# Seven block products in place of eight for f 6 to 16 only, in the first three feed-forwards of a two-layer diffusion step

## The chip, the cores and the metric

The kernel runs on one core of one Trainium2 chip. The metric is the time of one execution on the device in microseconds. A profile of one execution gives the times of single instructions; its span runs from the first to the last instruction. TensorE multiplies matrices, VectorE, ScalarE and GpSimd work on elements, SyncE's queue issues the transfers.

## The reference, cut to what matters

Two layers over 640 tokens (128 context, 512 latent) of width 1024. Each layer has a half-step feed-forward, a token mixer (attention in the first layer, Fourier mixing in the second) and another half-step feed-forward, so there are four feed-forwards of inner width 2816.

```python
def modulate(x, shift, scale):
    return x * (1.0 + scale[:, None, :]) + shift[:, None, :]

def swiglu(h, w_gate, w_up, w_down):
    return (jax.nn.silu(h @ w_gate) * (h @ w_up)) @ w_down

def half_ffn(x, shift, scale, gate, w_gate, w_up, w_down, g, b):
    h = modulate(x, shift, scale)
    return post_norm(x, FFN_HALF * swiglu(h, w_gate, w_up, w_down), gate, g, b)
```

The shifts, scales and gates are nine vectors a layer, each a product of the conditioning vector with a 1024 x 1024 part of `w_ada`.

## The kernel before, in words

The whole step is one program. Activations lie transposed: features on the 128 partitions, the 640 tokens along the row, in two halves (half 0 of 254 or 256 columns, half 1 of 386 or 384). Every float32 product is made of three: each operand is split into a high part (rounded to the matrix format) and a low part (the rest), and high x high, high x low and low x high are summed in PSUM (`mm3`, line 506). A high part is a cast, mostly on ScalarE; a low part is a subtraction on VectorE or GpSimd.

The method `ffn` (line 962) writes one feed-forward. The inner width is 22 blocks f of 128 columns. They are taken in groups (`THREES`, line 38): f 0 to 2, 3 to 5, 6 to 8, 9 to 11, 12 to 14, 15 and 16, 17 and 18, 19 to 21. The list `units` is the order of TensorE's work:

- `gk` and `g`: gate or up product of a block in the plain form, for one half, over the 8 row blocks of the weights. One block needs four such units, 4 x 24 matrix products.
- `s`: gate and up of a block for all tokens in seven block products in place of eight (Strassen's scheme in Winograd's form, `strassen`, line 1370). Gate and up of two row halves make a 2 x 2 block matrix with the two token halves of 320 columns. Seven products of 4 x 3 matrix products each; the weights need four sums and seven splits (`weights`), the activations the factors T1 to T4, made once (`form`), and the results five operations on VectorE before the low part of the hidden value (`gate_a`, `up_b`, `gate_b`, `kept`).
- `d`: down projection of a whole group for some of the 8 output blocks; it reads the hidden values (tiles `hd`), and VectorE adds it into `ya` with the gate (`add_out`).

Before the change a block is taken in the seven-product form if it is neither among the first three or four nor among the last two: f 4 to 19 in the first feed-forward, f 3 to 19 in the other three. Group g's down projection follows the first block of the next group. A list of loads with due times (`todo`) feeds four raw buffers through SyncE's queue. In the first three feed-forwards it also holds the loads of the modulation weights (40, 32 and 40 of 512 KB). Each is read twice on VectorE (`matvec`, line 538: the rows `junk<-raw,cond,bada`, followed by a read of the accumulator). The last feed-forward has none of them.

The order on each engine is fixed when the program is written: a planner with a clock per engine (`Queue`, line 179, `step`, line 404) hands each waiting piece of work to the engine that would have it done first. `end_t` is the unit from which loads for the next stage may start and late weights may use spare tiles; the last group's first down projection is preceded by the affine of the next stage (`affine`, line 622), which needs the modulation vectors of that stage.

Of the kernel before, what the change touches and what calls it, by code (L numbers as in the profile page):

```python
# [12 lines left out]
F32R = mybir.dt.float32r  # L13
# [10 lines left out]
NT = NP + NS  # L24
# [11 lines left out]
FT = DFF // 128  # L36

THREES = ((0, 3), (3, 3), (6, 3), (9, 3), (12, 3), (15, 2), (17, 2), (19, 3))
# [140 lines left out]
class Queue:  # L179
# [41 lines left out]
    def run(self, aps, outs, dur):  # L221
        c = self.clock
        t = max([self.t] + [self.after(x) for x in aps])
        outs = [x for x in outs if x is not None]
        for x in outs:
            t = max(t, c.free.pop(x.tensor.name, 0))
        self.t = t + dur
        for x in outs:
            c.written(x, self.t, self.name)
        for x in (*aps, *outs):  # L230
            c.in_use(x, self.t + 200)
# [51 lines left out]
class Step:  # L283
# [675 lines left out]
        place, when = lambda: ops.take(only=only), lambda: ops.free(2, only)  # L959
        return [(self.io["w_gu"][l, j, n // 2, n % 2], self.block(dst, n, place, when)) for n in range(m)]  # L960

    def ffn(self, l, j, i, nxt, pool, ops, gu, first, groups, ada=0, urgent=0, after=(), early=False, reserve=True, **kw):

# [11 lines left out]
        self.clock.exact(True)  # L977
        start, order = self.order, ORDER
        self.order = order
        plain = 4 if early else 3  # L980
        fast = lambda f: plain <= f < FT - 2
        last = len(groups) - 1
        units, held = [], []
        for g, (f0, n) in enumerate(groups):
# [5 lines left out]
            if g == last or g == 1 and not urgent:  # L990
                units, held = units + held, []
            for f in range(max(f0, 2 if early else 3), f0 + n):
# [4 lines left out]
                if f == f0:  # L997
                    units, held = units + held, []
# [11 lines left out]
        for t, u in enumerate(units):  # L1010
# [8 lines left out]
            for k in ks:  # L1019
                use.setdefault(k, [t, t])[1] = t  # L1020
            begins.append(begins[-1] + dur)
        fasts = [t for t, u in enumerate(units) if u[0] == "s"]
        end_t = fasts[-1] + 1

        tickets, graw, dn, wf, todo, dnx = deque(), {}, {}, {}, [], [0]

# [117 lines left out]
        for a in range(ada):  # L1144
            src, fn = self.ada_load()
            t = int(np.searchsorted(at, 0.95 * clock * (a + 0.5) / ada))
# [2 lines left out]
        todo.sort(key=lambda t: t[0])  # L1149
        gate = self.lnp.tile([128, KT, 2], F32, name="gate", bufs=2)  # L1150
        hid, hidden_by = {}, set()
        hids = Slots(pool, "hd", 2 * max(n for _, n in groups), [128, NT], F32R)
        sts, here, ready = [{}, {}], [0], []
        h, xs = self.h, self.xs
        self.ada_live = 0
# [26 lines left out]
        forms, formed = {}, []  # L1182
# [166 lines left out]
        pending = []  # L1349
# [11 lines left out]
        def flush(n=2):  # L1361
            while pending and n:
                fn, *args = pending.pop(0)
                fn(*args)
                n -= 1
            if formed and not pending and here[0] >= end_t:
                self.xt.give(*formed)
                formed.clear()

        def strassen(f):  # L1370
            st = {}
            st["b1"] = self.take()[:, :HALF]
            product(st["b1"], f, "A11", b11, True)
            self.spawn(snap(st, "p1", st["b1"]), first=1)
            st["b2"] = self.take()[:, :HALF]
            product(st["b2"], f, "S1", t1, True)
            flush(1)
            self.need(lambda: "p1" in st)
            product(st["b1"], f, "S2", t2, False)
            self.spawn(snap(st, "u2", st["b1"]), first=1)  # L1380
            st["b3"] = self.take()[:, :HALF]
            product(st["b3"], f, "A12", b21, True)
            self.spawn(gate_a(f, st), first=1)
            flush(1)
            self.need(lambda: "u2" in st)
            product(st["b1"], f, "S3", t3, False)
            self.spawn(up_b(st), first=1)
            pending.extend([(p4, f, st), (p3, f, st)])
# [18 lines left out]
        for t, u in enumerate(units):  # L1407
            here[0] = t
            half = u[1]
            n = self.n[half]  # L1410
# [6 lines left out]
            elif u[0] == "g":  # L1417
# [7 lines left out]
                else:  # L1425
                    self.spawn(hidden(u[2], half, pg, ps))
                flush()
            elif u[0] == "s":
                strassen(u[2])
            else:  # L1430
                _, _, outs, g = u
# [981 lines left out]
    def run(self):  # L2413
        io = self.io
        got = {}
        with ExitStack() as ctx:
            spill = ctx.enter_context(self.tc.tile_pool(name="spill", bufs=1, space=bass.MemoryType.DRAM))
            saved = [spill.tile([128, NT], F32, name=f"sp{o}") for o in range(KT)]
            psums = ExitStack()
            self.psum(psums)  # L2420
            self.ada_open(ctx)
            with ExitStack() as sctx:
                self.x_slots(sctx)
                pool = self.ffn_pool(sctx)
                ops = self.work_slots(pool, 10, True)
                self.start(ops)
                free_w = lambda: sum(map(is_w, ops.rest)) == 4 or bool(got)
                after = [(io["w_ab"][n], self.block(got, n, self.wtile, free_w)) for n in range(2)]
                after += [(io["w_ab"][n], lambda t, n=n: got.update({n: t})) for n in (2, 3)]
                self.ffn(0, 0, 0, (0, 3), pool, ops, {}, 0, THREES, 40, 8, after, True, spill=saved, kept=False)  # L2430
            got, old = {}, got
            self.spawn(self.ada_beside(16), first=-2)
            self.mixer_ab(old, got, psums)
            fin = {}
            self.psum(ctx)
            self.x_slots(ctx)
            with ExitStack() as sctx:
                pool = self.ffn_pool(sctx)
                ops = self.work_slots(pool, 10, False)
                old = {}  # L2440
                self.ab_out(1, 0, ops, saved, self.first_blocks(0, 1, old, ops, 5), got, ORDER[::-1])
                got = {}
                self.ffn(0, 1, 2, (1, 0), pool, ops, old, 5, THREES, 32, 0, self.first_blocks(1, 0, got, ops, 2, is_w))
                self.ffn(1, 0, 3, (1, 3), pool, ops, got, 2, THREES, 40, after=[self.fin_block(n, fin) for n in range(3)], reserve=False, plain=True)
            with ExitStack() as sctx:
                fx = self.pool(sctx, "fx")
                parts = self.mixer_f(fin, fx)
                pool = self.ffn_pool(sctx)
                ops = self.work_slots(pool, 10, False)
                got = {}  # L2450
                self.f_out(4, 1, parts, fx, ops, self.first_blocks(1, 1, got, ops, 5))
                self.ffn(1, 1, 5, None, pool, ops, got, 5, THREES, reserve=False)
                self.drain()

def layouts(inputs):
# [144 lines left out]
```

## Time and profile before

| | us |
|---|---|
| median of 3 runs | 2534.91 |
| lowest and highest run | 2534.05, 2539.28 |
| profiled execution | 2540.61 |
| its span | 2538.7 |
| TensorE busy with products | 2343.9 |
| VectorE busy | 2091.6 |
| ScalarE busy | 1006.7 |
| GpSimd busy | 641.1 |

Busy times are sums over the span of the profiled execution; the stages of the program differ in what limits them, so the shares of a stretch say more than those of the whole. In tables by stretch the columns give the busy time of an engine with its number of instructions in brackets, the granted TensorE clock as a share of full speed, and the transfers. In lists in order of time the columns are start, duration, engine, line, operation, output and inputs, shapes and count; brackets give the idle time just ahead and who ended it.

### The profile page before, as it was taken

The page shows a single profiled execution, that of the slowest core. Times are in us where ns is not written, and L with a number is a line of the kernel's source. Part 1 is how long each engine was busy: PE and PEld are TensorE (multiplying, and loading weights), DVE is VectorE, ACT ScalarE, POOL GpSimd, SP SyncE. Part 2 cuts the span into 40 slices and gives each one's busy share as a digit, 9 for nine tenths or more (in the row PEclk, how much of TensorE's full clock was granted, in tenths as well). Part 3 has the DMA queues.
Part 4 walks back from the last instruction along what each step waited for, and adds up shares of the span by engine and source line. Part 5 has one row for each costly group of instructions (what it writes and reads, how often), then busy time and mean ns, then how long its engine had stood idle before and what let it go on. Part 6 is the DMA issues. An engine that isn't in the chain of part 4 may idle for free. (4 is left out here: it accounts for less than half of the span.)

```text
span 2538.7 us, 40214 instructions
## 1 busy us (share of the span) xinstructions
PE 2343.9 (92%) x14909; PEld 2231.7 (88%) x14909; DVE 2091.6 (82%) x4254; ACT 1006.7 (40%) x2212; POOL 641.1 (25%) x601
## 2 busy tenths in 40 slices
PE   7899999889989998999999889999996998999997
PEld 6899999888668898999998889999985788999996
DVE  7878888879767778889887898889889788777766
ACT  3333434243556634434442434333324344444432
POOL 7501012252322333011221621011325552000001
PEclk7999999989799998999999989999997999999998
DMA  6423333523122211433334033333334201222211
GB/s 243 133 84 117 117 125 125 161 85 112 46 59 68 72 66 63 133 117 117 119 123 133 25 117 119 114 126 116 119 115 163 96 33 60 76 87 88 90 61 42
DMA packets 98564, 258.03 MB, mean 102 GB/s; under 512 B 15224, under 2 KB 28216, under 8 KB 98368
## 3 DMA queue, kind: packets, MB, share of 16 engines
q1 hardware_dynamic: 98368, 255.45, 30.9%
q8 instruction: 118, 1.93, 0.3%
q14 instruction: 78, 0.64, 0.1%
HBM read 247.79 MB, written 5.52 MB: 100 GB/s over the span
## 5 line engine op out<-in xcount | busy, mean ns | idle before, releaser
L463 PE MATMUL a<-hh,wu 128*128 128x320 f32 (+4 forms) x2312 | 555.3, 314 | 14.0 <-POOL wu L200 7.9
L463 PE MATMUL a<-hd,wu 128*128 128x386 f32 (+3 forms) x2712 | 468.1, 316 | 24.0 <-DVE tmp L200 8.5
L200 ACT CAST wu<-raw 128x512 fp32r<-128x512 f32 (+1 forms) x482 | 303.0, 650 | 431.4 <-DVE raw L200 149.4
L463 PEld LDWEIGHTS a<-hd,wu 128*128 128x128 f32 x2712 | 424.0, 193 | 27.8 <-DVE tmp L200 9.0
L463 PEld LDWEIGHTS a<-hh,wu 128*128 128x128 f32 x2312 | 404.7, 192 | 16.5 <-POOL wu L200 8.2
L463 PE MATMUL a<-xt,wu 128*128 128x320 f32 (+2 forms) x2456 | 392.1, 313 | 19.8 <-ACT tmp L200 9.9
L463 PEld LDWEIGHTS a<-xt,wu 128*128 128x128 f32 x2456 | 369.3, 190 | 26.8 <-ACT tmp L200 13.6
L200 DVE CUSTOM_DVE_ANT_0 junk<-raw,cond,bada 128x1024 bf16<-128x1024 f32 x256 | 358.9, 1402 | 23.0 <-DMA raw<-in_w_ada 20.7
L463 PE MATMUL a<-hl,wu 128*128 128x320 f32 (+4 forms) x1140 | 357.9, 314 | 8.9 <-POOL hl L200 7.8
L200 DVE SCALAR_TENSOR_TENSOR ya<-a,gate,ya 128x128 f32<-128x128 f32 (+3 forms) x768 | 298.2, 432 | 70.6 <-PE a L463 67.1
L200 DVE TENSOR_TENSOR wu<-raw,wu 128x512 fp32r<-128x512 f32 (+1 forms) x412 | 309.4, 762 | 29.1 <-ACT wu L200 25.6
L463 PE MATMUL a<-hh,w 128*128 128x320 f32 (+6 forms) x1056 | 266.0, 318 | 2.1 <-ACT hh L200 2.1
L463 PE MATMUL a<-hd,w 128*128 128x254 f32 (+3 forms) x1320 | 247.2, 314 | 12.2 <-ACT hd L200 9.1
L200 POOL TENSOR_TENSOR wu<-raw,wu 128x512 fp32r<-128x512 f32 (+1 forms) x70 | 112.4, 1611 | 516.6 <-ACT wu L200 370.0
L463 PEld LDWEIGHTS a<-hl,wu 128*128 128x128 f32 x1140 | 218.9, 192 | 10.9 <-POOL hl L200 8.6
L463 PEld LDWEIGHTS a<-hd,w 128*128 128x128 f32 x1320 | 209.3, 191 | 13.9 <-ACT hd L200 9.8
L200 ACT CAST w<-raw 128x512 fp32r<-128x512 f32 (+3 forms) x222 | 139.9, 638 | 179.1 <-DVE raw L200 52.6
L463 PEld LDWEIGHTS a<-hh,w 128*128 128x128 f32 (+1 forms) x1056 | 186.5, 191 | 5.9 <-ACT hh L200 3.4
L200 POOL TENSOR_TENSOR w<-raw,w 128x512 fp32r<-128x512 f32 (+3 forms) x58 | 86.6, 1495 | 403.6 <-ACT w L200 361.3
L463 PE MATMUL a<-hl,w 128*128 128x320 f32 (+6 forms) x544 | 172.1, 316 | 1.8 <-POOL hl L200 1.6
L463 PE MATMUL a<-xt,w 128*128 128x320 f32 (+2 forms) x1016 | 166.3, 314 | 5.1 <-ACT tmp L200 5.1
L463 PEld LDWEIGHTS a<-xt,w 128*128 128x128 f32 x1016 | 154.5, 192 | 8.3 <-ACT tmp L200 6.3
(443 smaller groups left out, 3446.2 us busy)
## 6 DMA issues: line engine op xcount, KB each, us to landing
raw<-in_w_gu SPq DMA_DIRECT2D x176, 512.0 KB, 4.4
raw<-in_w_ada SPq DMA_DIRECT2D x128, 512.0 KB, 3.7
raw<-in_w_dn SPq DMA_DIRECT2D x176, 256.0 KB, 3.1
raw<-in_w_fin SPq DMA_DIRECT2D x16, 520.0 KB, 4.5
raw<-in_w_ab SPq DMA_DIRECT2D x11, 512.0 KB, 4.5
xt<-in_w_ada SPq DMA_DIRECT2D x8, 512.0 KB, 7.5
raw<-in_w_abo SPq DMA_DIRECT2D x8, 512.0 KB, 4.0
raw<-in_w_fout SPq DMA_DIRECT2D x8, 512.0 KB, 4.1
```

The lines of the kernel that those rows point to most:

```text
L200: return getattr(self.engine, op)(*args, **kw)
L463: pe.engine.matmul(out, w, x, **kw)
```

## The change

A new parameter `seven` names the blocks that are taken in the seven-product form: f 6 to 16 where nothing is said, f 3 to 19 in the call for the last feed-forward. In the first three, f 3 (or 4) to 5 and f 17 to 19 become plain units. `end_t` is now taken from the first unit of f 19, whatever its form, and the factors of the blocks are given back after the last seven-product block. The number of hidden tiles is written as 6, which it was.

```diff
-    def ffn(self, l, j, i, nxt, pool, ops, gu, first, groups, ada=0, urgent=0, after=(), early=False, reserve=True, **kw):
+    def ffn(self, l, j, i, nxt, pool, ops, gu, first, groups, ada=0, urgent=0, after=(), early=False, reserve=True, seven=(6, 17), **kw):
...
-        plain = 4 if early else 3
-        fast = lambda f: plain <= f < FT - 2
+        fast = lambda f: seven[0] <= f < seven[1]
...
-        fasts = [t for t, u in enumerate(units) if u[0] == "s"]
-        end_t = fasts[-1] + 1
+        seven_t = max(t for t, u in enumerate(units) if u[0] == "s") + 1
+        end_t = min(t for t, u in enumerate(units) if u[0] in "gs" and u[2] == FT - 3) + 1
...
-        hids = Slots(pool, "hd", 2 * max(n for _, n in groups), [128, NT], F32R)
+        hids = Slots(pool, "hd", 6, [128, NT], F32R)
...
-            if formed and not pending and here[0] >= end_t:
+            if formed and not pending and here[0] >= seven_t:
...
-                self.ffn(1, 1, 5, None, pool, ops, got, 5, THREES, reserve=False)
+                self.ffn(1, 1, 5, None, pool, ops, got, 5, THREES, reserve=False, seven=(3, FT - 2))
```

The order of the instructions moves on every engine, since the planner places all of them anew. Three places follow.

TensorE, second feed-forward, where the down projection of group 0 (it reads the hidden tiles `hd`) ends and block f 3 begins (it reads the activations' high and low parts `hh` and `hl`). Before:

```order
L463 MATMUL a_10654<-hd_10217,w_10313 128x386
L463 MATMUL a_10654<-hd_10218,w_10313 128x386
L463 MATMUL a_10654<-hd_10217,w_10313 128x386
L463 MATMUL a_10667<-hh_78,wu_10366 128x320
L463 MATMUL a_10667<-hl_86,wu_10366 128x320
L463 MATMUL a_10667<-hh_78,wu_10366 128x320
```

Now:

```order
L463 MATMUL a_10578<-hd_10162,w_10258 128x386
L463 MATMUL a_10578<-hd_10163,w_10258 128x386
L463 MATMUL a_10578<-hd_10162,w_10258 128x386
L463 MATMUL a_10590<-hh_78,wu_10309 128x386
L463 MATMUL a_10590<-hl_86,wu_10309 128x386
L463 MATMUL a_10590<-hh_78,wu_10321 128x386
```

Block f 3 starts with a product of half 1 (386 columns) with a high and a low weight tile of their own, where a product of 320 columns with one tile for both parts stood.

VectorE, third feed-forward, ahead of the first down projection of the last group: from the low part of the second last hidden product to that of the last (`ISA junk` is a modulation product, `ISA mod` its accumulator, `affa` and `affb` the affine of the next stage). Before:

```order
L200 TENSOR_TENSOR hd_19254<-tmp_19245,hd_19253 128x386
L200 ISA junk,mod_8_14753<-raw_19201,cond,bada 128x1024
...
L200 ISA junk,mod_8_14753<-raw_19267,cond,bada 128x1024
...
L200 ISA junk,mod_8_14753<-raw_19287,cond,bada 128x1024
...
L200 TENSOR_SCALAR affa<-mod_4_14749 128x16
...
L200 TENSOR_TENSOR tmp_19320<-tmp_19320,a_19282 128x386
L200 ISA junk,mod_8_14753<-raw_19309,cond,bada 128x1024
L200 ISA mod_8_14753 128x1
L200 TENSOR_TENSOR hd_19352<-tmp_19320,hd_19351 128x386
```

Now:

```order
L200 ISA junk,mod_8_14632<-raw_19006,cond,bada 128x1024
L200 ISA mod_8_14632 128x1
L200 TENSOR_TENSOR tmp_19084<-tmp_19084,a_19058 128x386
L200 TENSOR_TENSOR hd_19092<-tmp_19084,hd_19091 128x386
L200 TENSOR_TENSOR raw_19141<-raw_19141 128x2x256
L200 TENSOR_TENSOR raw_19143<-raw_19143 128x520
L200 TENSOR_TENSOR raw_19145<-raw_19145 128x2x256
L200 TENSOR_TENSOR tmp_19150<-tmp_19150,a_19116 128x386
L200 TENSOR_SCALAR affa<-mod_4_14628 128x16
```

The five modulation products between the two hidden products and the one behind the last multiplication are gone from there: the last one of the feed-forward now stands ahead of the second last hidden product. Three sums of the next stage's weights have come in, and the affine stands behind the last multiplication; its low part is on GpSimd.

VectorE, third feed-forward, ahead of the first output of group 0's down projection: from the low part of the second last hidden product of half 0 to the last. Before:

```order
L200 TENSOR_TENSOR hd_15105<-tmp_15297,hd_15104 128x254
L200 TENSOR_TENSOR wu_15314<-raw_15292,wu_15314 128x512
L200 TENSOR_TENSOR raw_15292<-raw_15292 128x512
L200 TENSOR_TENSOR raw_15290<-raw_15292,raw_15290 128x512
...
L200 TENSOR_TENSOR wu_15362<-raw_15290,wu_15362 128x512
L200 TENSOR_TENSOR wu_15373<-raw_15292,wu_15373 128x512
L200 TENSOR_TENSOR wu_15375<-raw_15290,wu_15375 128x512
L200 TENSOR_TENSOR raw_15290<-raw_15290,raw_15292 128x512
L200 TENSOR_TENSOR tmp_15383<-tmp_15383,a_15300 128x254
...
L200 TENSOR_TENSOR hd_15152<-tmp_15383,hd_15151 128x254
```

Now:

```order
L200 TENSOR_TENSOR hd_14984<-tmp_15181,hd_14983 128x254
L200 TENSOR_TENSOR xt_15216<-tmp_15088,xt_15216 128x320
L200 TENSOR_TENSOR xt_15216<-tmp_15089,xt_15216 128x320
L200 ISA junk,mod_4_14628<-raw_15240,cond,bada 128x1024
L200 ISA mod_4_14628 128x1
L200 TENSOR_TENSOR tmp_15247<-tmp_15247,a_15174 128x254
```

The sums and low parts of the weights of block f 3 are gone; the low parts of the factors (`xt`) have come together there.

## Rows read from the trace of the kernel before

**Rows 1.** The page's first part: busy us, share of the span, instructions.

```profile
PE 2343.9 (92%) x14909; PEld 2231.7 (88%) x14909; DVE 2091.6 (82%) x4254; ACT 1006.7 (40%) x2212; POOL 641.1 (25%) x601
```

**Rows 2.** Busy times by stretch: the four feed-forwards behind group 0, in their order.

```profile
core 0: us, PE busy (x) PEld busy (x) DVE busy (x) ACT busy (x) POOL busy (x), PEclk, DMA share, GB/s
136.00:526.00 390.00, 369.76 (x2460) 365.39 (x2458) 333.01 (x625) 139.54 (x274) 59.44 (x45) 0.98 0.37 120
1019.00:1409.00 390.00, 380.03 (x2545) 376.85 (x2543) 334.21 (x638) 144.78 (x286) 62.58 (x45) 0.99 0.36 119
1505.00:1908.00 403.00, 385.63 (x2543) 381.58 (x2542) 348.03 (x652) 141.93 (x284) 64.84 (x49) 0.97 0.36 119
2137.00:2516.00 379.00, 376.93 (x2550) 374.83 (x2548) 268.63 (x529) 141.59 (x285) 22.57 (x17) 1.00 0.22 72
```

**Rows 3.** TensorE in order of time: the two ends of the last feed-forward's stretch.

```profile
2137.43 0.31 PE L463 MATMUL a<-hh,wu 128*128 128x320 f32 x1
...
2515.31 0.52 PE L463 MATMUL a<-hd,wu 128*128 128x254 f32 x3
```

**Rows 4.** TensorE in order of time: 36 products of 320 columns and the next one.

```profile
327.19 5.44 PE L463 MATMUL a<-xt,wu 128*128 128x320 f32 x36
332.47 0.31 PE L463 MATMUL a<-hh,w 128*128 128x320 f32 x1
```

**Rows 5.** TensorE in order of time: waits in the first and third feed-forward.

```profile
343.29 0.56 PE L463 MATMUL a<-xt,wu 128*128 128x320 f32 x2 [3.61 <-ACT wu L200]
...
490.96 0.69 PE L463 MATMUL a<-hd,xt 128*128 128x384 f32 x1 [6.86 <-ACT hd L200]
...
1482.53 0.58 PE L463 MATMUL a<-hd,w 128*128 128x254 f32 x1 [6.25 <-ACT hd L200]
...
1869.69 0.44 PE L463 MATMUL a<-hd,w 128*128 128x386 f32 x1 [2.90 <-ACT hd L200]
```

**Rows 6.** VectorE in order of time, ahead of the last of these waits' end.

```profile
1864.42 2.19 DVE L200 CUSTOM_DVE_ANT_0 junk<-raw,cond,bada 128x1024 bf16<-128x1024 f32 x1
...
1868.54 0.55 DVE L200 TENSOR_TENSOR tmp<-tmp,a 128x386 f32<-128x386 f32 x1
1869.01 1.28 DVE L200 CUSTOM_DVE_ANT_0 junk<-raw,cond,bada 128x1024 bf16<-128x1024 f32 x1
...
1870.21 1.61 DVE L200 TENSOR_TENSOR hd<-tmp,hd 128x386 fp32r<-128x386 f32 x1
```

**Rows 7.** Busy times by stretch (columns of rows 2): behind that wait, and undisturbed.

```profile
1870.00:1880.00 10.00, 8.26 (x32) 8.12 (x32) 7.13 (x12) 0.00 (x0) 1.91 (x2) 0.66 0.18 52
2200.00:2210.00 10.00, 10.00 (x66) 10.00 (x65) 9.26 (x22) 3.01 (x6) 0.00 (x0) 1.00 0.08 33
```

**Rows 8.** VectorE's groups by form: busy us, mean ns, then idle before.

```profile
L200 DVE TENSOR_TENSOR wu<-raw,wu 128x512 fp32r<-128x512 f32 x387 | 276.0, 724 | 26.2 <-ACT wu L200 24.3
L200 DVE TENSOR_TENSOR raw<-raw,raw 128x512 f32<-128x512 f32 x181 | 129.9, 718 | 16.7 <-DMA raw<-in_w_gu 11.3 <-issue 1.6 <-POOL raw L200 1.2
L200 DVE TENSOR_TENSOR tmp<-a,tmp 128x320 f32<-128x320 f32 x201 | 97.9, 488 | 53.6 <-PE a L463 42.6 <-ACT tmp L200 9.8
L200 DVE TENSOR_TENSOR hd<-tmp,hd 128x320 fp32r<-128x320 f32 x125 | 63.1, 513 | 10.2 <-ACT hd L200 9.9
L200 DVE TENSOR_TENSOR wu<-raw,wu 128x1024 fp32r<-128x1024 f32 x25 | 33.5, 1355 | 2.9 <-PE a L463 1.6 <-ACT wu L200 1.3
L200 DVE TENSOR_TENSOR hd<-tmp,hd 128x386 fp32r<-128x386 f32 x14 | 10.3, 735 | 4.0 <-ACT hd L200 3.9
L200 DVE TENSOR_TENSOR tmp<-tmp,a 128x386 f32<-128x386 f32 x15 | 8.2, 550 | 8.2 <-PE a L463 8.2
```

**Rows 9.** Waits, longest in total, from 440 to 505 us: ScalarE for a load.

```profile
ACT w L200 <- DMA raw<-in_w_ab: 6.9, 2, 5.6
```

**Rows 10.** The page's part on DMA issues: KB each, us to landing.

```profile
raw<-in_w_gu SPq DMA_DIRECT2D x176, 512.0 KB, 4.4
```

## The prediction, made before the change was run

> **What bounds the kernel now.** I read the profile's first part, then a table of the four feed-forwards by stretch of time, then the rows that end TensorE's waits inside them. The first part gives no clear owner: matrix products are busy 92% of the span, weight loads 88%, VectorE 82% [rows 1]. The table does [rows 2]. Each of its stretches runs from the first product after group 0's down projection to the last product of the last group. The last feed-forward has the same units as the second and third, but no modulation products beside it, and its stretch lasts 379 us at a granted clock of 1.00; its two ends are in [rows 3]. The second takes 390 us, the third 403. The first starts one seven-product block later, which is 84 products of 320 columns at (332.47 - 327.19) / 36 = 0.147 us [rows 4], or 12.3 us; so its measure is 367 us, and it takes 390. Against the undisturbed stretch the three lose 23 + 11 + 24 = 58 us. VectorE's busy share of the undisturbed time tells why: 269 / 379 = 71% in the last, but 333 / 367 = 91%, 334 / 379 = 88% and 348 / 379 = 92% in the first three. TensorE needs all the time there, VectorE nearly all.
>
> TensorE's own waits agree: 3.61 us for a cast weight in mid-stage, 6.86 and 2.90 us for the last hidden product [rows 5]. What stood ahead of that hidden product in the third feed-forward is in VectorE's rows: a modulation product of 2.19 us, the eight small operations of the next affine, the multiplication itself only at 1868.54, another modulation product, and only then its low part [rows 6]. TensorE had been ready since about 1866.8. Such a wait costs twice: in the 10 us around it TensorE got through 32 products at a clock of 0.66, against 66 at 1.00 in a full stretch [rows 7].
>
> **What the change costs.** A block in the seven-product form takes 7 x 12 = 84 products of 320 columns; in the plain form 48 of 384 or 386 columns and 48 of 256 or 254, 30,720 columns for 26,880. That is 12 products of 320 more, 12 x 0.147 = 1.76 us [rows 4]. Seventeen blocks change: f 4, 5, 17, 18, 19 in the first feed-forward (f 2 and 3 were plain), f 3 to 5 and 17 to 19 in the second and third. The instruction order has 204 products more, which agrees. **+29.9 us** on TensorE. I count all of it, since TensorE has no spare time in those stretches.
>
> **What it takes from VectorE.** A seven-product block has 4 weight sums, 7 low parts of 512 columns, 5 operations on products and 2 low parts of the hidden values: 4 x 0.718 + 7 x 0.724 + 5 x 0.488 + 2 x 0.513 = 11.4 us. A plain one has 2 low parts of 1024, 2 multiplications and 2 low parts of the hidden values, at most 2 x 1.355 + 2 x 0.550 + 2 x 0.735 = 5.3 us [rows 8]. That is 6.1 us a block if all of it stands on VectorE. Some of both stands on GpSimd, whose order has 44 instructions fewer. In VectorE's order 155 instructions go; form by form with the means of the trace that is 70 us, some 23 us a feed-forward. ScalarE has 141 instructions fewer and is busy 40% of the span [rows 1]: worth nothing. The transfers are the same 715 issues; what moves is when the modulation loads come.
>
> If 19 of the 23 us lie inside the stretch, VectorE's share of the time that TensorE now needs (376, 389 and 389 us) falls to 84%, 81% and 84%. The four stretches of before give 0 us lost at 71%, 11 at 88%, 23 and 24 at 91 and 92%. A straight line from the first to the second gives 6 to 9 us at the new shares; the points bend upward beyond, so a little less is likely: I take 6 each. **58 - 18 = 40 us come back.** The ends: all 58 come back (the last feed-forward's level), or none.
>
> The end of each stretch is the surest part. In the order of before, six modulation products and the affine stand between the last two hidden products; after the change all of them stand ahead of the second last, and what is left in front of the last one is a few casts or sums of weights. The 6.86 and 2.90 us should shrink to the chain's own latency of one to three. The clock comes back with them.
>
> **The start of the third feed-forward.** TensorE waits 6.25 us there for the last hidden product of group 0 [rows 5]. Between the last two hidden products' low parts VectorE's order now lacks 4 low parts of weights and 3 weight sums, 4 x 0.724 + 3 x 0.718 = 5.1 us, and gains up to 2 us in larger pieces of the factors' and weights' splits moved ahead of it. I take **-3 us**, between 0 and -5. The second feed-forward shows no such wait, and the first waits there for its eight urgent modulation products, which stay.
>
> The last feed-forward keeps its seven-product blocks. The factors of the blocks are given back after f 16, so late down-projection weights find room sooner (96 more of their products read such a slot): nothing, since no wait of before is for a slot.
>
> **Sum.** +29.9 - 40 - 3 = -13 us. The profiled execution took 2540.6 us (span 2538.7 and 1.9 around it), so it would be 2527. It was 5.7 us above the median of the three runs, 2534.9, from which **2521 us** follows. Some 0.2% (5 us) is what a measurement of this kernel can tell from no change.
>
> **A rule against the change.** In VectorE's share I see the cause, though TensorE's weight loads have the higher share of the span, 88% to 82% [rows 1], and 382 of 403 us of the third stretch [rows 2]. The Trainium skill (Perfetto Trace Analysis, Identifying the Most-Contended Engine) says to judge TensorE by the share of its weight loads and VectorE by its busy time, and to work on the engine with the highest first. By it, adding products to TensorE brings only their 29.9 us.
>
> **Rivals.**
> - *TensorE bounds these stretches, and the waits are latency.* A hidden product passes from TensorE through ScalarE, VectorE, ScalarE and VectorE again before the down projection can read it, in the plain form as in the other. If the waits at the heads of groups come from that chain and not from VectorE's queue, they stay, and the change costs up to 29.9 us: 2565 us. It decides where fewer than 30 us of the 58 come back. Against it: the last feed-forward has the same chain and loses nothing. Chance 0.10. It is the case that the skill's rule describes.
> - *A transfer takes the modulation's place.* In the new order VectorE's casts, low parts or sums of the next stage's weights stand right ahead of the last hidden product, and each waits for its load. Such a load was late by 5.6 us on ScalarE before [rows 9], where it blocked nobody; 512 KB take 4.4 us to land [rows 10]. In the order the up product of f 20, 48 products of 386 columns with its gate (some 8 us at the rate of [rows 4]), lies between the release of a raw buffer and that place and should hide it. Also, between the first outputs of the groups of f 15 and f 17 up to 11 modulation products now stand: VectorE's order times the means gives some 30 us there, TensorE's work 27.6 us. Then some 13 us each stay lost: 58 - 39 = 19 come back, +29.9 - 19 - 3 = +8: 2543 us. Chance 0.20.
> - *All lost time comes back*, to the level of the last feed-forward: 29.9 - 58 - 5 = -33: 2502 us. Chance 0.12.
>
> That the change doesn't do what it says is excluded by the order: the blocks named are plain in it, 204 products more.
>
> **How the numbers follow.** My forecast has 0.58. Its own range is 2513 to 2534 (between 3 and 10 us left in each stretch). The range takes in the best case and the second rival, **2502 to 2544**; what is left out is the first rival's upper part and the tails. Faster by over 5 us: 0.53 of my forecast, all of the best case, 0.02 of the second rival, **0.67**. Within 5 us: 0.05 + 0.07 + 0.02 = **0.14**. Slower: 0.11 + 0.08 = **0.19**.
>
> **What would show it.** Right: the three stretches last about 382, 395 and 395 us (undisturbed 376, 389, 389 and 6 each), the last stays at 379; no modulation product stands between the multiplication and the low part of the last hidden product, and TensorE's wait there is under 3 us; VectorE's total falls by some 60 us or more, TensorE's count of products rises by 204. Wrong: stretches of over 400 us, with waits on loads or on ScalarE's casts at the heads of the last groups, or granted clocks of 0.66 still there.

## The result, and the profile after

The changed kernel takes 2501.56 us (median of four runs, 2494.91 to 2504.22), the kernel before beside it 2536.71 us (2534.05 to 2539.28): ratio 0.9858, 95% interval 0.9834 to 0.9881. That is 35 us less. Faster was forecast, but 13 to 14 us, and the measured time lies just under the lower end of the range. Measured again later, the same two gave 0.9837 [0.9812, 0.9862].

The profiled execution has a span of 2501.3 us, against 2538.7. The page's first part, which answers to [rows 1]:

```profile
PE 2356.0 (94%) x15113; PEld 2248.9 (90%) x15113; DVE 2011.3 (80%) x4099; ACT 948.5 (38%) x2071; POOL 574.2 (23%) x557
```

TensorE has 204 products more, as the order said, and VectorE is busy 80 us less (70 were forecast). The four feed-forwards behind group 0, in the columns of [rows 2]:

```profile
131.00:509.00 378.00, 372.11 (x2520) 369.55 (x2519) 313.44 (x581) 123.04 (x238) 56.44 (x44) 1.00 0.38 123
1005.00:1397.00 392.00, 388.91 (x2618) 386.91 (x2616) 311.33 (x588) 125.17 (x243) 45.12 (x34) 1.00 0.35 115
1488.00:1878.00 390.00, 387.37 (x2616) 384.78 (x2614) 326.86 (x613) 125.48 (x242) 52.41 (x38) 1.00 0.38 123
2100.00:2478.00 378.00, 376.10 (x2546) 374.21 (x2545) 268.37 (x528) 141.05 (x284) 22.56 (x17) 1.00 0.23 72
```

All four now have a granted clock of 1.00. The four waits in [rows 5] are gone or under 1 us. In the first feed-forward the last hidden product's low part now ends a wait of 0.16 us, where its high part ended one of 6.86:

```profile
476.95 4.28 PE L463 MATMUL a<-hd,xt 128*128 128x384 f32 x23 [0.16 <-POOL hd L200]
```

At the start of the third, the wait for the last hidden product of group 0, 6.25 us in [rows 5], is 0.76 us. The wait just ahead of it, for the second last hidden product, stays: 3.79 us before (first fence), 4.45 us after (second fence, which shows both).

```profile
1471.61 0.58 PE L463 MATMUL a<-hd,wu 128*128 128x254 f32 x1 [3.79 <-ACT hd L200]
```

```profile
1460.98 0.58 PE L463 MATMUL a<-hd,wu 128*128 128x254 f32 x1 [4.45 <-ACT hd L200]
...
1466.54 2.07 PE L463 MATMUL a<-hd,w 128*128 128x254 f32 x8 [0.76 <-POOL hd L200]
```

At the end of the third, VectorE stood idle 4.97 us ahead of the multiplication that [rows 6] had at 1868.54, and the affine now runs behind it while GpSimd makes the low part; no modulation product stands there. The second fence below is the 10 us that answer to [rows 7]: 57 products at a clock of 1.00 in place of 32 at 0.66, of 386 columns in both.

```profile
1842.87 0.56 DVE L200 TENSOR_TENSOR tmp<-tmp,a 128x386 f32<-128x386 f32 x1 [4.97 <-PE a L463]
1843.35 0.17 DVE L200 TENSOR_SCALAR affa<-mod 128x16 f32<-128x16 f32 x1
```

```profile
1843.00:1853.00 10.00, 10.00 (x57) 9.68 (x56) 7.62 (x19) 0.51 (x1) 0.91 (x1) 1.00 0.00 0
```

With the ends taken from the first and last product, as the prediction did, the program divides so (us; a start runs from the first hidden value that a down projection reads to the beginning of the stretch). In the first feed-forward group 0's down projection stands behind block f 3, in the other three ahead of it, so the first stretch has one block less.

| part | before | after | difference |
|---|---|---|---|
| first start | 32.1 | 27.4 | -4.7 |
| first stretch | 390.0 | 378.1 | -11.9 |
| second start | 21.2 | 21.2 | 0 |
| second stretch | 389.9 | 391.6 | +1.7 |
| third start | 37.6 | 31.7 | -5.9 |
| third stretch | 403.5 | 390.0 | -13.5 |
| fourth start | 31.7 | 30.1 | -1.6 |
| fourth stretch | 378.4 | 378.4 | 0 |
| everything else | 854.3 | 852.8 | -1.5 |

Above what TensorE needs undisturbed (374.9, 389.0 and 389.0 us with the forecast's price), 3, 3 and 1 us are left in the three stretches, where 24, 12 and 25 were lost before. Measured lengths put the need a little lower. With the same units and no modulation products the last feed-forward takes 387.5 us (the kernel that has the plain blocks there too, below), and the first stretch of the kernel with f 8 to 14, which has four more plain blocks in it, takes 379.3 us, so that at the forecast's price at most 372.3 are needed without them. By these about 6, 4 and 3 us are left.

### The profile page after: what moved, and what is told of

The parts are those of the page before. It is cut to its first block, busy times and chain, and to the rows that moved or that the text cites. A ratio compares the mean times of both kernels' runs of the same rounds, so it can differ in the third digit from the quotient of the medians.

```text
span 2501.3 us, 40294 instructions
## 1 busy us (share of the span) xinstructions
PE 2356.0 (94%) x15113; PEld 2248.9 (90%) x15113; DVE 2011.3 (80%) x4099; ACT 948.5 (38%) x2071; POOL 574.2 (23%) x557
## 3 DMA queue, kind: packets, MB, share of 16 engines
q1 hardware_dynamic: 98368, 255.45, 31.7%
## 5 line engine op out<-in xcount | busy, mean ns | idle before, releaser
L463 PE MATMUL a<-hh,wu 128*128 128x254 f32 (+4 forms) x2856 | 689.2, 315 | 13.4 <-POOL wu L200 7.8
L463 PEld LDWEIGHTS a<-hh,wu 128*128 128x128 f32 x2856 | 501.4, 192 | 15.7 <-POOL wu L200 8.1
L463 PE MATMUL a<-hl,wu 128*128 128x320 f32 (+4 forms) x1356 | 426.0, 314 | 8.6 <-POOL hl L200 7.7
L463 PE MATMUL a<-hh,w 128*128 128x320 f32 (+6 forms) x1192 | 311.2, 317 | 2.1 <-ACT hh L200 2.1
L463 PE MATMUL a<-xt,wu 128*128 128x320 f32 (+2 forms) x1868 | 294.2, 310 | 4.2 <-ACT tmp L200 4.2
L463 PEld LDWEIGHTS a<-xt,wu 128*128 128x128 f32 x1868 | 277.5, 188 | 7.5 <-ACT tmp L200 5.9
L463 PEld LDWEIGHTS a<-hl,wu 128*128 128x128 f32 x1356 | 260.5, 192 | 10.9 <-POOL hl L200 8.5
L463 PE MATMUL a<-hd,w 128*128 128x386 f32 (+3 forms) x1200 | 223.3, 313 | 4.3 <-POOL hd L200 1.7
L200 ACT CAST hd<-tmp 128x320 fp32r<-128x320 f32 (+4 forms) x176 | 79.1, 459 | 227.3 <-DVE tmp L200 185.4
L200 DVE TENSOR_TENSOR tmp<-tmp,a 128x320 f32<-128x320 f32 (+4 forms) x126 | 61.0, 484 | 95.9 <-PE a L463 89.2
```

Source lines behind the costliest of these rows:

```text
L200: return getattr(self.engine, op)(*args, **kw)
L463: pe.engine.matmul(out, w, x, **kw)
```

## Experiments

All stretches below are read in the same way; ratios are to the kernel before, run beside each on the same chip. In the edits, three dots stand for the rest of a line.

| kernel | seven products for f | ratio [95%] | first, second, third stretch |
|---|---|---|---|
| changed | 6 to 16 | 0.9858 [0.9834, 0.9881] | 378.1, 391.6, 390.0 |
| e1 | 6 to 19 | 0.9913 [0.9884, 0.9942] | 384.6, 391.1, 391.9 |
| e2 | 3 (4) to 16 | 0.9923 [0.9896, 0.9949] | 382.6, 392.9, 390.7 |
| e3 | as before, narrow modulation | 0.9749 [0.9714, 0.9784] | 378.3, 382.8, 385.0 |
| e4 | 6 to 16, VectorE loaded | 1.0224 [1.0188, 1.0260] | 402.9, 413.4, 421.9 |
| e5 | 5 to 17 | 0.9929 [0.9908, 0.9949] | 394.2, 387.6, 396.8 |
| e6 | 8 to 14 | 0.9888 [0.9871, 0.9906] | 379.3, 395.0, 395.0 |
| e7 | 6 to 16, last one too | 0.9891 [0.9874, 0.9908] | 377.0, 390.5, 391.3 |
| e8 | 6 to 16, second as before | 0.9852 [0.9835, 0.9869] | 377.8, 390.2, 392.5 |
| e9 | 6 to 16, second 5 to 17 | 0.9826 [0.9805, 0.9847] | 376.3, 388.9, 391.6 |
| e10 | 6 to 17 | 0.9926 [0.9905, 0.9948] | 385.8, 393.5, 401.4 |
| e11 | 5 to 16 | 0.9868 [0.9841, 0.9896] | 384.1, 388.3, 391.3 |
| e12 | 6 to 16 again | 0.9837 [0.9812, 0.9862] | 377.4, 391.1, 391.1 |

### Each end of the change alone

```diff
-    ... reserve=True, seven=(6, 17), **kw):
+    ... reserve=True, seven=(6, 20), **kw):
```

> Plain blocks only ahead (f 3 to 5; f 4 and 5 in the first feed-forward), f 17 to 19 back in the seven-product form: 8 plain blocks instead of 17, so 14.1 us of TensorE's work over the kernel before. Theory 'VectorE's queue, by place' (the waits at the end of a feed-forward come from the modulation products and splits that stand there): the end waits stay (6.9, 5.4 and 2.9 us before the last hidden product, clocks of 0.66), the stretches behind group 0 last some 385, 392 and 398 us, the whole some 2525 to 2535. Rival 'backlog from the start' (what VectorE falls behind in group 0 and 1 is carried to the end): nearly all lost time comes back too, stretches of some 372, 386 and 386, the whole about 2495.

```diff
-    ... reserve=True, seven=(6, 17), **kw):
+    ... reserve=True, seven=(3, 17), **kw):
```

(and 4 to 16 in the call for the first feed-forward)

> Plain blocks only behind (f 17 to 19), f 3 to 5 (4 and 5 in the first feed-forward) back in the seven-product form: 9 plain blocks, 15.8 us of TensorE's work over the kernel before. Theory 'VectorE's queue, by place': the end waits go, the stretches last some 377, 386 and 390 us, the waits at the start of the first and third feed-forward stay (7.3 us before group 0's last outputs in the first, 6.3 in the third); the whole some 2500 to 2512. Rival 'backlog from the start': stretches of 385, 392, 398 and more, the whole 2525 or more.

Measured: 2517.02 us and 2517.23 us; each part brings about 20 to 22 us. The starts belong to the part ahead: 26.4 and 31.8 us with it, 31.8 and 37.7 without it, as before. In the stretches both parts bring time back, so neither theory holds alone. What separates them is where the waits stand. TensorE's waits of the kernel with the part ahead in the first feed-forward, then of the one with the part behind:

```profile
478.06 0.69 PE L463 MATMUL a<-hd,xt 128*128 128x384 f32 x1 [5.87 <-ACT hd L200]
```

```profile
342.90 0.56 PE L463 MATMUL a<-xt,wu 128*128 128x320 f32 x2 [3.61 <-ACT wu L200]
```

The part ahead leaves the late wait of [rows 5] for the last hidden product and takes the wait in mid-stage for a cast weight; the part behind does the reverse, and there the wait in mid-stage is as long as before to the hundredth of a microsecond. The start of the first feed-forward, from 104 us to the beginning of its stretch, shows which wait goes there. TensorE's waits before (us in total, times, longest), and after; the longest is 3.3 us in the kernel with the part ahead and 7.3 in the one with the part behind:

```profile
PE a L463 <- DVE tmp L200: 8.5, 2, 7.3
```

```profile
PE a L463 <- DVE ya L200: 3.2, 1, 3.2
PE a L463 <- DVE tmp L200: 1.0, 1, 1.0
```

### Less and more work on VectorE, in an unchanged order

The first of these is the kernel before with modulation products that read 128 of 1024 columns (they leave out the rest of the sum); the planner reckons with the whole width, so the order is that of before. The second is the changed kernel with an unused product of 320 columns behind each modulation product.

```diff
-                self.matvec(self.mods[l, m], self.bada[:, l, m, o:o + 1], o, raw, v)
+                self.matvec_narrow(self.mods[l, m], self.bada[:, l, m, o:o + 1], o, raw, v)
```

> The kernel before with the same order on every engine, but each modulation product beside the feed-forwards and the mixers reads 128 of its 1024 columns (the rest of the sum is left out), so that it takes some 0.3 us instead of 1.4 on VectorE. TensorE's work, the loads and all waits stay as they are. Theory 'VectorE's share': the three stretches fall to the undisturbed length, some 367 to 371, 379 to 383 and 379 to 383 us, and the whole to 2475 or less. Rival 'latency of the hidden chain or late loads': they stay within 5 us of 390, 390 and 403, the whole above 2520.

```diff
                 self.matvec(self.mods[l, m], self.bada[:, l, m, o:o + 1], o, raw, v)
+                self.nc.vector.engine.tensor_tensor(self.junk[:, :320], raw[:, :320], self.cond[:, v, :320], ALU.mult)
```

> The changed kernel with the same order, and behind each modulation product beside the feed-forwards a further VectorE multiplication of 320 columns (some 0.4 us, result unused): 32, 26 and 32 us more on VectorE in the three feed-forwards with the same work on TensorE. Theory 'VectorE's share': the share goes back to some 92, 88 and 93%, and the lost time comes back: the stretches grow by some 20, 8 and 25 us from 378, 392 and 390, the whole to 2545 or more. Rival 'the order, not the amount' (what helped is that the modulation products no longer stand ahead of the last hidden product): the stretches grow by under 6 us each, the whole stays under 2525.

Measured: 2475.08 us, ratio 0.9749, and 2595.61 us, ratio 1.0224. VectorE's groups by form, of the narrow products and of the added ones (the products of before take 1402 ns):

```profile
L548 DVE CUSTOM_DVE_ANT_0 junk<-raw,cond,bada 128x128 bf16<-128x128 f32 x256 | 108.1, 422 | 20.8 <-DMA raw<-in_w_ada 18.7
```

```profile
L553 DVE TENSOR_TENSOR junk<-raw,cond 128x320 bf16<-128x320 f32 x256 | 150.9, 590 | 8.9
```

The first three stretches by busy time (columns of [rows 2]), narrow products, then loaded:

```profile
125.00:503.00 378.00, 367.35 (x2457) 363.37 (x2455) 272.20 (x624) 138.71 (x274) 53.53 (x45) 0.99 0.38 124
986.00:1369.00 383.00, 379.06 (x2547) 376.87 (x2546) 281.76 (x634) 144.81 (x287) 55.06 (x44) 0.99 0.37 121
1463.00:1848.00 385.00, 378.70 (x2545) 375.46 (x2543) 280.54 (x652) 142.27 (x284) 58.87 (x49) 1.00 0.38 124
```

```profile
139.00:542.00 403.00, 379.98 (x2520) 375.01 (x2518) 345.29 (x644) 122.24 (x237) 61.27 (x45) 0.98 0.36 115
1044.00:1458.00 414.00, 396.59 (x2620) 392.63 (x2618) 339.95 (x648) 124.87 (x243) 45.48 (x34) 0.98 0.34 110
1548.00:1970.00 422.00, 398.89 (x2617) 394.30 (x2615) 365.29 (x688) 124.27 (x242) 50.01 (x38) 0.97 0.35 114
```

VectorE's load is a cause: taking some 250 us of it over the whole program brings 64 us, and giving 151 us to the changed kernel costs 93 (ratio 1.0224 against 0.9858, of 2537 us). Its three stretches grew by 25, 22 and 32 us, where 20, 8 and 25 were expected.

But the late waits did not come back with the load. The fences show TensorE's longest wait in the last 80 us of the first stretch, before and in the loaded kernel, where it is the only one listed; in the last 80 us of its second and third stretch none is listed. Its waits of 3 to 6 us all lie earlier. So the late waits of before hang on the order.

```profile
PE a L463 <- ACT hd L200: 6.9, 1, 6.9
```

```profile
PE a L463 <- POOL hd L200: 0.2, 1, 0.2
```

A smaller load does not mend everything either. The narrow kernel still loses 12 us in its first stretch, with VectorE at 74% of the undisturbed 366 us; the last feed-forward loses nothing at 71%. The wait in mid-stage is unchanged in it. Its place on all four engines (TensorE, VectorE, GpSimd, ScalarE):

```profile
328.26 0.56 PE L463 MATMUL a<-xt,wu 128*128 128x320 f32 x2 [3.61 <-ACT wu L200]
```

```profile
323.82 0.49 DVE L200 TENSOR_TENSOR tmp<-tmp,tmp 128x320 f32<-128x320 f32 x1 [1.55 <-ACT tmp L200]
324.23 0.48 DVE L200 TENSOR_TENSOR tmp<-a,tmp 128x320 f32<-128x320 f32 x1
324.63 0.68 DVE L200 TENSOR_TENSOR wu<-raw,wu 128x512 fp32r<-128x512 f32 x1
325.23 0.48 DVE L200 TENSOR_TENSOR hd<-tmp,hd 128x320 fp32r<-128x320 f32 x1
326.86 0.69 DVE L200 TENSOR_TENSOR raw<-raw,raw 128x512 f32<-128x512 f32 x1 [1.15 <-POOL raw L200]
```

```profile
325.53 1.30 POOL L200 TENSOR_TENSOR raw<-raw 128x512 f32<-128x512 f32 x1 [45.60 <-DVE wu L200]
```

```profile
327.59 1.14 ACT L200 CAST wu<-raw 128x512 fp32r<-128x512 f32 x2 [2.42 <-DVE raw L200]
```

Here a low part of a weight (324.63) stands in VectorE's order behind the operations on the preceding block's product, for which VectorE itself waits (idle 1.55 us). GpSimd's sum of weights waits for that low part, the next sum on VectorE for GpSimd, ScalarE's cast for that sum, TensorE for the cast: 0.68 + 1.30 + 0.69 + 0.57 us (half of ScalarE's pair) with the hand-overs between them. No engine is overloaded at that moment: GpSimd, VectorE and ScalarE each stand idle for over 1 us ahead of their part. The sums were written into the order too late, and a faster VectorE does not mend it.

### One block less and one block more

```diff
-    ... reserve=True, seven=(6, 17), **kw):
+    ... reserve=True, seven=(5, 18), **kw):
```

> The changed kernel with the seven-product form for f 5 to 17 in the first three feed-forwards: 6 of the 17 blocks go back to it (TensorE 6 x 1.76 = 10.6 us less, VectorE some 6 x 4.7 = 28 us more). Theory A (lost time grows smoothly with VectorE's load, some 29 us left with half of the blocks changed, 7 with all): some 19 to 21 us are left in the three stretches with 11 of 17 changed, 13 more than in the changed kernel, so the whole is within 5 us of it (+1 to +4). Theory B (there is a point in the load from which nothing is lost, and the changed kernel is beyond it): lost time stays under 10 us, stretches of about 375, 388 and 387 us, the whole 7 to 11 us faster than the changed kernel, about 2492.

```diff
-    ... reserve=True, seven=(6, 17), **kw):
+    ... reserve=True, seven=(8, 15), **kw):
```

> The changed kernel with the seven-product form for f 8 to 14 only: 12 more plain blocks, 21 us more on TensorE, some 56 us less on VectorE. The changed kernel has 6.8 us left in the three stretches and 10 us over the least start (21.2 us to the end of group 0's down projection) in the first and third. Theory A and B agree if VectorE's load is the whole cause: stretches of 382, 396 and 396 us without loss, starts at most 5 us better, whole +10 to +20, about 2515. If the waits in starts and between stretches still come from VectorE, these shrink too and the whole is only 0 to +8.

Measured: 2521.55 us (ratio 0.9929), 18 us slower than the changed kernel by the ratios, and 2512.92 us (0.9888), some 8 us slower. With six blocks put back (f 5 and 17 in each of the three) the kernel has returned halfway, and the first stretch, 394.2 us, is longer than before: neither a smooth growth with the load nor a safe level below a point, so both theories fall. With twelve more plain blocks the second and third stretch take 395.0 us and TensorE is busy 394.3 of it: there nothing is left to bring back, and each further block only costs. Its starts, 26.6 and 31.6 us, are about those of the changed kernel, so they do not go on shrinking with VectorE's load.

### The two blocks apart

```diff
-    ... reserve=True, seven=(6, 17), **kw):
+    ... reserve=True, seven=(6, 18), **kw):
```

> The changed kernel with f 6 to 17 in the seven-product form in the first three feed-forwards: only f 17 goes back. Theory of places (each block in the seven-product form next to the ends brings back waits at its own place): in the first stretch TensorE's wait some 350 us in (6.0 us for the last hidden product with f 5 to 17, 6.9 before) is there again, the waits 140 to 220 us in stay away; stretches of about 386, 389 and 391 us, the whole +4 to +8 against the changed kernel. Theory of load (a smooth function of VectorE's total): a sixth of the way back, lost time 7 to 9 us more in all three, spread over the stretches, 5.3 us less on TensorE: whole +2 to +4.

```diff
-    ... reserve=True, seven=(6, 17), **kw):
+    ... reserve=True, seven=(5, 17), **kw):
```

> The changed kernel with f 5 to 16 in the seven-product form in the first three feed-forwards: only f 5 goes back. Theory of places: in the first stretch the waits for a cast or a sum of weights 140, 200 and 220 us in are there again (2.2, 3.9 and 1.1 us not busy with f 5 to 17), in the third that at 210 to 230; the ends stay as in the changed kernel; first stretch 385 to 390, second 389 to 391, third 392 to 394, whole +5 to +12. Theory of load: lost time spread, whole +2 to +4 as with f 17 put back, and the two kernels alike.

Measured: 2522.45 us and 2509.00 us, beside 2499.59 for the changed kernel on the same chip. VectorE has the same load in both. The page's first part, f 17 put back, then f 5:

```profile
PE 2358.0 (94%) x15077; PEld 2249.0 (89%) x15077; DVE 2031.8 (81%) x4144; ACT 959.2 (38%) x2096; POOL 561.0 (22%) x547
```

```profile
PE 2358.9 (94%) x15077; PEld 2246.9 (90%) x15077; DVE 2030.6 (81%) x4130; ACT 958.3 (38%) x2095; POOL 582.2 (23%) x562
```

A smooth function of the load cannot give 23 us for one and 9 for the other. The places do. With f 5 put back, the wait in mid-stage of the first feed-forward is there again, and the stretches and the whole come within 1 us of what the theory of places had (the wait that it expected in the third, at 210 to 230 us, did not come back):

```profile
342.05 0.90 PE L463 MATMUL a<-xt,wu 128*128 128x320 f32 x2 [3.61 <-ACT wu L200]
```

With f 17 put back, the first feed-forward has its late wait again, as expected:

```profile
480.64 0.66 PE L463 MATMUL a<-hd,xt 128*128 128x384 f32 x1 [3.44 <-ACT hd L200]
```

In the third, modulation products and the affine stand again ahead of the last hidden product's multiplication on VectorE (the second row is the first of the affine's eight operations), with one more modulation product ahead of the low part. TensorE waits there in two pieces, and the granted clock of the 10 us is 0.66 (third fence, in the columns of [rows 2]). The expectation had +4 to +8 us in all: it was right for the first stretch (386, and 385.8 came), but it did not name this place and kept the third stretch at 391, which took 401.4.

```profile
1851.71 2.18 DVE L200 CUSTOM_DVE_ANT_0 junk<-raw,cond,bada 128x1024 bf16<-128x1024 f32 x1
...
1855.15 1.26 DVE L200 TENSOR_SCALAR affa<-mod 128x16 f32<-128x16 f32 x1
...
1857.37 0.56 DVE L200 TENSOR_TENSOR tmp<-tmp,a 128x386 f32<-128x386 f32 x1
1857.84 2.01 DVE L200 CUSTOM_DVE_ANT_0 junk<-raw,cond,bada 128x1024 bf16<-128x1024 f32 x1
```

```profile
1858.58 0.44 PE L463 MATMUL a<-hd,xt 128*128 128x386 f32 x1 [2.63 <-ACT hd L200]
1860.38 1.97 PE L463 MATMUL a<-hd,xt 128*128 128x386 f32 x5 [1.36 <-DVE hd L200]
```

```profile
1858.00:1868.00 10.00, 8.06 (x28) 7.80 (x29) 5.80 (x9) 0.51 (x1) 0.77 (x1) 0.66 0.15 54
```

### The last feed-forward, and the second

```diff
-    ... got, 5, THREES, reserve=False, seven=(3, FT - 2))
+    ... got, 5, THREES, reserve=False)
```

> The changed kernel with seven products for f 6 to 16 only in the last feed-forward too: 6 more plain blocks where VectorE has no modulation products and its share is 71%. If the gain comes from VectorE's load alone: the last stretch goes from 378.4 to 389 us (6 x 1.76 = 10.6 more), nothing comes back, the whole about +10, some 2512. If plain blocks at the ends of a stretch were better whatever the load (shorter chain at the heads of groups), the last stretch stays under 384 and the whole gains or loses under 5.

Measured: 2512.82 us, ratio 0.9891, 8 us slower than the changed kernel by the ratios. The stretch goes from 378.4 to 387.5 us. Its row, beside the last of [rows 2]:

```profile
2095.00:2482.00 387.00, 386.88 (x2618) 385.18 (x2616) 238.69 (x474) 123.32 (x242) 16.95 (x13) 1.00 0.21 67
```

TensorE is busy 386.88 - 376.93 = 10.0 us longer for six blocks, 1.66 each, and the stretch is 9.1 us longer, 1.5 each (forecast 1.76). Where no time is lost, the plain form only costs.

```diff
-    ... self.first_blocks(1, 0, got, ops, 2, is_w))
+    ... self.first_blocks(1, 0, got, ops, 2, is_w), seven=(3, FT - 2))
```

> The changed kernel with the second feed-forward as it was (f 3 to 19 in the seven-product form), the first and third changed. The second stretch gained nothing from the change (389.9 before, 391.6 after: 10.6 us more need, 9 less lost). If each stretch stands by itself: its body goes back to about 390, the way from the first to the second stretch to 472 to 475, the third stays at 390 and its start at 31.7; whole within 3 us of the changed kernel. Rival: VectorE's queue carries its backlog over into the next stage, so that the way to the third and its start are late again by 2 to 6 us, whole +2 to +6.

Measured: 2502.44 us, ratio 0.9852 [0.9835, 0.9869]: not to be told from the changed kernel. In the second feed-forward the change neither gains nor loses; the whole gain comes from the first and third.

```diff
-    ... self.first_blocks(1, 0, got, ops, 2, is_w))
+    ... self.first_blocks(1, 0, got, ops, 2, is_w), seven=(5, 18))
```

> The changed kernel, with the second feed-forward alone at f 5 to 17 in the seven-product form. Where all three had f 5 to 17, the second stretch took 387.6 us (391.6 in the changed kernel) with 1.2 to 3 us lost, the first and third 394.2 and 396.8. If each feed-forward stands by itself: first stretch 378, second 388, third 390, the whole 4 us faster than the changed kernel (about 0.2%). If the order of one stage shifts the next (start and stretch of the third as with the second feed-forward put back: 29.7 and 392.5), the gain is 0 to 4.

> The changed kernel itself once more, beside the others on one chip: stretches within 1 us of those of its first profile (378.1, 391.6, 390.0, 378.4) if its order alone sets them; ratio to before 0.983 to 0.988.

Measured on one chip: 2496.60 us for the mix (0.9826) and 2499.59 us for the changed kernel (0.9837 [0.9812, 0.9862]). The mix has the lowest median of all kernels that compute the whole output, but the intervals overlap: whether it beats the changed kernel stays open. In the changed kernel run again every engine has the same order of operations as the first time. The repeated profile has stretches of 377.4, 391.1 and 391.1 us, as expected, but its starts are 29.2 and 29.7 us (27.4 and 31.7 the first time) and its way from the first stretch to the second start 468.8 us (474.5). So a few microseconds outside the stretches are not evidence from one profile.

## Why the prediction came out as it did

- **Cause and sign** were right. VectorE's order, with modulation products and an affine ahead of hidden products, held TensorE up in the first three feed-forwards; the waits went where the prediction said that they would ("the end of each stretch is the surest part").
- **TensorE's price** was nearly right: 204 products more, 1.5 to 1.66 us a block where 1.76 was forecast, so 26 to 28 us in all in place of 29.9.
- **VectorE's relief** was right in size: 80 us less where the order gave 70, and shares of 84, 80 and 84% of the undisturbed time where 84, 81 and 84% were forecast.
- **"I take 6 each" failed.** In the prediction's own terms 3, 3 and 1 us are left, 7 in place of 18; by the measured lengths above about 13. The three stretches together went from 1183.4 to 1159.7 us, -24 where the forecast had +29.9 - 40 = -10. The straight line through lost time over VectorE's share was the wrong rule. With f 17 back, shares of 86, 83 and 87% went with stretches 8, 2 and 10 us longer than those of e12, and with f 5 back, shares of 85, 81 and 86% with stretches 7 us longer, 3 shorter and the same; the narrow kernel lost 12, 4 and 7 us at 74%. The lost time is a sum of a few waits at named places, each of which depends on what the order puts ahead of one instruction and on how long that takes. The prediction had read two such places in the order and then priced the remainder by an average. Its comparison in [rows 7] also made the clock look dearer than it is: the 32 products have 386 columns, the 66 beside them 254 and 320, and 57 of 386 columns pass in 10 us at a clock of 1.00. No term of its sum rests on that.
- **The starts and ways between** were counted as -3 us and gave about -14: starts -12.2, the rest -1.5, of which a few us are the spread of one profile. "The first waits there for its eight urgent modulation products, which stay" failed: the longest wait fell from 7.3 to 3.2 us, and that is the part ahead, since the kernel with the part behind alone keeps 31.8 us and the one with the part ahead alone has 26.4. Modulation products do count there too: with all of them narrow the start is 21.2 us. The third start's -3 was -5.9 in the first profile: the 6.25 us that the prediction read went down to 0.76, more than the 5 us that the order gave. The start is 29.7 to 32.0 us in all kernels without f 3 and 4 in the seven-product form, against 37.6 and 37.7 with them (35.2 with narrow modulation products).
- **The rivals.** "All lost time comes back" (2502 us, chance 0.12) is what happened in the measured time, 2501.56, though not by its terms: 7 us or more stayed in the stretches, and the starts gave more than its 5. That the time agrees with it to half a microsecond is luck. "TensorE bounds these stretches" fell: the chain of a hidden product has the same five steps after the change (the last of them, the low part, on GpSimd), and its wait is 0.16 us. By the Trainium skill (Perfetto Trace Analysis, Identifying the Most-Contended Engine) the engine with the highest share is to be optimized first, which was TensorE with weight loads at 88% against VectorE's 82%. Taken as a call to relieve TensorE, the rule does not fit the measurement: adding to the engine with the higher share and relieving the one with the lower made the kernel 35 us faster. "A transfer takes the modulation's place" did not occur: none of TensorE's waits in the first and third stretch of after that the trace lists is longer than 1.52 us.

What stays open: the way from the third stretch to the last start is 192 to 195 us in the kernels whose f 18 and 19 are plain in the third feed-forward, and 194.5, 197.4 and 202.2 us in the three where they are not. How much of the 5.2 us by which it became shorter is the change's, the runs do not settle.

## What to carry to other kernels

Here an engine with a fixed order feeds the bound engine, and lost time was not a function of the feeder's share. In such a case count it wait by wait, and for each ask whether the instruction waited for stands behind work (then less load or another order helps) or behind another engine's result (then only the order does). With the same load, f 17 back in the seven-product form in three stages cost 23 us, and f 5 cost 9. A form that is cheaper on the bound engine can be dearer as a whole at such a place and still pay elsewhere: with f 6, 7, 15 and 16 plain too the kernel was some 8 us slower.

## What the runs showed of the hardware that was not expected

The modulation product over 128 columns takes 422 ns, that over 1024 columns 1402 ns in the kernel before: an eighth of the columns takes three tenths of the time. The same instruction over 1024 columns took 1.28 us in most places and 2.01 to 2.19 us in some of the lines shown; which neighbour lengthens it was not tried.
